# Sums of gated pairs, on GpSimd and VectorE or by accumulating transfers in DRAM

## The chip, the cores and the metric

The kernel runs on one core of a Trainium2 chip. A core has TensorE (PE in the profile, matmuls, with its weight loads PEld), VectorE (DVE), ScalarE (ACT) and GpSimd (POOL); SyncE (SP) issues the transfers in the kernel before. The metric is the device time of one execution in microseconds, lower is better.

## The reference

One encoder layer with shared weights is run on a prompt of 512 tokens and on a sample of 1024 tokens, in float32. After windowed attention, a convolution module and the output projection, both go through a gated feed-forward block, and this is the part that the change touches:

```python
h = _rmsnorm(x, norm_ffn_g[l])
u = _dwconv(h @ w_up[l], ffn_dw_w[l], ffn_dw_b[l])
x = x + (jax.nn.silu(u[..., :D_FF]) * u[..., D_FF:]) @ w_down[l]
...
return _rmsnorm(x, norm_final_g)
```

D_MODEL is 1024 and D_FF is 2816, which is 22 blocks of 128 columns. The output has to agree with this to nearly float32, so every matmul operand is split into a high part (float32r) and a low part (the rest), and each product is three matmuls: high by high, high by low, low by high.

## The kernel before

**Two feed-forward stages and one common last product.** The prompt's up-projection is a plain product: `ffn_step(k)` (line 1033) runs for each of the 22 blocks k, with two groups of 24 matmuls (lines 347, 348 and 350), the splitting of the next weights (`split`, line 227: the high half on ACT at line 230, the low half on GpSimd at line 231), the three taps of the convolution on DVE (line 969) and `gate(k)`. Meanwhile the sample's attention is woven in from a list of side jobs. Then follows the sample's output projection (lines 840 to 842), with transposes for norms (lines 816 and 1152) and further side jobs. The sample's up-projection is computed with seven products of half-size blocks in place of eight (Strassen's scheme in Winograd's form): `first` to `seventh` (lines 1307 to 1352), twelve matmuls each (lines 1229 to 1231). The down-projection (lines 1579 to 1581) is done for prompt and sample together, by the same scheme.

**The sums of a pair.** The seven products of the down-projection want, as their stationary operand, three blocks of the gated values as they are and four sums of blocks. Two neighbouring blocks of D_FF columns form a pair, 11 pairs in all. Call the even block's left and right token halves eL and eR, the odd block's oL and oR. Products 1, 2 and 4 use eL, oL and oR. Product 5 uses eR + oR, product 7 uses eL - eR, product 6 uses eR + oR - eL, and product 3 uses oL - (eR + oR - eL).

**Prompt.** `gate` (line 992) finishes a tile of 128 x 512 by a multiplication on GpSimd (line 1000), or on DVE for every fourth block, and stores it to `gt` in DRAM (line 1001). For pairs 7, 8 and 9 the sums are made at once by `pair_sums` (line 1013); for pairs 0 to 6 and the last one, `pair_sums` is a side job of the sample's output projection: it loads the pair again from `gt` (line 1016), makes four subtractions or additions of 128 x 256 on GpSimd (lines 1023, 1025, 1027, 1029) and stores the four results to `gb` (line 1030). The same GpSimd queue holds the two small operations of each norm's factor (`rstd_of`, lines 214 and 215).

**Sample.** The loop over j (line 1715) runs products of blocks j and j + 1 in a fixed order of TensorE's instructions: second(j), sixth(j), first(j+1), seventh(j), fifth(j+1), fourth(j), third(j). Between them stand the splits of the next block's weights (`split_up`, line 1200: high part on ACT at line 1215, low part on GpSimd through line 1092; split 7 reads a sum from a 2 KB tile), `value_part(j-1)` and `gate_part(j)`. `gate_part` takes the gate half through the convolution (lines 1357 to 1359) and a tanh (line 1366); `value_part` makes the gated product (line 1376), takes the value half through the convolution and multiplies (line 1378) into t, 128 x 1024. An even block's t is kept to the next step, and its left half is stored to `ga` (line 1383). With an odd block two halves are stored (line 1387), DVE makes the four sums of 128 x 512 (through lines 1089 and 1092), into the tiles x and e and a small one y, and SP stores them (line 1393). Copies of ACT between products (lines 1312, 1321, 1330, 1342) seed and drain the accumulators.

**Tiles.** `Slots` (line 74) gives out buffers of fixed classes: 15 q of 4096 bytes per partition, 4 c of 4224, 61 h of 2048, and some small ones. A request takes the smallest class that fits, and in it the buffer that came free first in program order. An instruction that writes a buffer waits until all that used it before, transfers included, have finished. `split_up` takes one 4 KB tile for high and low part if a q or c is free, and two h otherwise. Six of the q are reserved for the raw weights in the sample's stage.

**Order.** Where nothing is fixed by hand, a planner sets each engine's order of instructions at build time, by priority and by the times that it assumes; each engine then works through its own list in order. In the sample's up-projection TensorE's order is by hand, in the last product SP's too.

**The down-projection.** `load_next` (line 1491) fetches the operands ahead, from `ga` (line 1517), from `gt` or `gb` (lines 1512 and 1513) and from w_down. `evacuate` (line 1595) adds up the products as they end: u starts as product 1, o11 is u + product 2, e is product 5; then u takes product 6, o12 is u + e; u takes product 7, e takes u; u takes product 4. Product 3 goes into o12 at the end.

Of the kernel before, what the change touches and what calls it, by code (L numbers as in the profile page):

```python
# [9 lines left out]
F32 = mybir.dt.float32  # L10
# [3 lines left out]
ALU = mybir.AluOpType  # L14

P = 128
D = 1024
KC = D // P
NT = 512
# [154 lines left out]
def tile_hybrid_encoder(ctx: ExitStack, tc: tile.TileContext, xs, xsT, rel_bias, norm_attn_g, w_in,  # L174
                        attn_sink, w_out, norm_ffn_g, w_up, w_down, norm_final_g, packed, onehot, outs):
    nc = tc.nc
# [5 lines left out]
    dr = ctx.enter_context(tc.tile_pool(name="dr", bufs=1, space=bass.MemoryType.DRAM))  # L182
# [8 lines left out]
    sb = Slots(lambda tag: homes[tag[0]], dict(q=(15, 4096), c=(4, 4224), h=(61, 2048), d=(2, 2176), s=(32, 64)), "q", KEEP)  # L191
# [19 lines left out]
    ended = {}  # L211
# [99 lines left out]
    side, pace = deque(), dict(rate=0.0, due=0.0, conv=0.0, credit=0.0, late=0.0)  # L311
# [673 lines left out]
    NPAIR = NJ // 2  # L985
    HT = NT // 2
    gt = [dr.tile([P, 2, NT], F32, name=f"gt{p}") for p in range(NPAIR)]
    gb = [dr.tile([P, 4, HT], F32, name=f"gb{p}") for p in range(NPAIR)]
    GB = {5: 0, 7: 1, 6: 2, 3: 3}
    HL, HR = slice(0, HT), slice(HT, NT)  # L990

    def gate(j, a, b):
        th, t = bank("gate"), sb.tile([NT])
        nc.scalar.activation(th[:], a[:], AF.Tanh, scale=0.5)
        if j % 4 == VG:
            nc.vector.scalar_tensor_tensor(th[:], th[:], 1.0, a[:], op0=ALU.add, op1=ALU.mult)
            nc.vector.tensor_tensor(t[:], th[:], b[:], op=ALU.mult)
        else:
            nc.vector.scalar_tensor_tensor(t[:], th[:], 1.0, a[:], op0=ALU.add, op1=ALU.mult)
            nc.gpsimd.tensor_tensor(t[:], t[:], b[:], op=ALU.mult)  # L1000
        nc.sync.dma_start(gt[j // 2][:, j % 2, :], t[:])
        if j // 2 < SOON or j // 2 == NPAIR - 1:
            return
        if j % 2 == 0:
            evens[j // 2] = t
        else:
            for _ in pair_sums(j // 2, evens.pop(j // 2), t):
                pass

    evens = {}  # L1010
    SOON = 7

    def pair_sums(p, e=None, o=None):
        if e is None:
            g = sb.tile([2, NT], among="c")
            nc.sync.dma_start(g[:], gt[p][:])
            yield 0.0
            yield 0.0
            e, o = g[:, 0, :], g[:, 1, :]
        r = sb.tile([4, HT], among="c")  # L1020
        gp = nc.gpsimd.tensor_tensor
        with tc.issue_after(ended["pool"]):
            gp(r[:, 0, :], e[:, HR], o[:, HR], op=ALU.add)
        yield 0.0
        gp(r[:, 1, :], e[:, HL], e[:, HR], op=ALU.subtract)
        yield 0.0
        gp(r[:, 2, :], r[:, 0, :], e[:, HL], op=ALU.subtract)
        yield 0.0
        gp(r[:, 3, :], o[:, HL], r[:, 2, :], op=ALU.subtract)
        nc.sync.dma_start(gb[p][:], r[:])  # L1030
        yield 0.0

    def ffn_step(k):
        want_up_raw(k + 1, 1)
# [50 lines left out]
    W2 = 2 * NT  # L1085
    L, R = slice(0, NT), slice(NT, W2)

    def add(out, a, b, eng=None):
        (eng or nc.vector).tensor_tensor(out, a, b, op=ALU.add)  # L1089

    def sub(out, a, b, eng=None):
        (eng or nc.vector).tensor_tensor(out, a, b, op=ALU.subtract)  # L1092
# [153 lines left out]
            yield 0.0  # L1246

    side.extend((right_halves(), conv_norm(4 + NE)))
    side.extend(pair_sums(p) for p in (*range(SOON), NPAIR - 1))
    pace.update(rate=2.2)  # L1250
    for i in range(4, NB - 2):
        if i + NE + 1 < NB:
# [40 lines left out]
    def wide():  # L1293
        return wide_banks.tile([W2])

    ga = {(i, p): dr.tile([P, NT], F32, name=f"ga{i}_{p}") for i in range(1, 8) for p in range(NPAIR)}
    st = {}

    def pair_banks(j):
# [65 lines left out]
        t = s["t"] = sb.tile([W2])  # L1365
        nc.scalar.activation(t[:], ug[:], AF.Tanh, scale=0.5)

    even = {}

    def value_part(j):  # L1370
        if j < 0:
            return
        p = j // 2
        s = st.pop(j)
        ug, t = s["ug"], s["t"]
        nc.vector.scalar_tensor_tensor(t[:], t[:], 1.0, ug[:], op0=ALU.add, op1=ALU.mult)
        uv = dwconv(s.pop("wy"), NJ + j)
        nc.vector.tensor_tensor(t[:], t[:], uv[:], op=ALU.mult)
        del ug, uv
        s.clear()  # L1380
        if j % 2 == 0:
            even[p] = t
            nc.sync.dma_start(ga[1, p][:], t[:, L])
            return
        e, x, y = even.pop(p), sb.tile([W2]), sb.tile([NT])
        for i, blk in ((2, L), (4, R)):
            nc.sync.dma_start(ga[i, p][:], t[:, blk])
        add(x[:, R], e[:, R], t[:, R])
        sub(x[:, L], e[:, L], e[:, R])
        sub(e[:, R], x[:, R], e[:, L])  # L1390
        sub(y[:], t[:, L], e[:, R])
        for i, b in ((5, x[:, R]), (7, x[:, L]), (6, e[:, R]), (3, y[:])):
            nc.sync.dma_start(ga[i, p][:], b)

# [94 lines left out]
    def load_next(n):  # L1491
        for _ in range(n):
            if ahead:
                key, p = ahead.popleft()
                roomy = sum(f[0][0] in "qc" for f in sb.free) > 5
                if (key, p) in second_half:
                    t = second_half.pop((key, p))
                elif key in BRIEF and p % 2 == 0 and p + 1 < NPAIR and roomy:
                    both = sb.tile([2, NT])
                    t, second_half[key, p + 1] = Part(both, 0), Part(both, 1)  # L1500
                    both = None
                else:
                    t = sb.tile([NT])
                pr[key, p] = t
                what, i, n2 = key
                if what == "a":
                    src = ga[i, p][:]
                elif what == "g":
                    n = min(2, NPAIR - 2 * p)
                    for q in range(n):  # L1510
                        j, h = {1: (0, HL), 2: (1, HL), 4: (1, HR)}.get(i, (0, None))
                        src = gb[2 * p + q][:, GB[i], :] if h is None else gt[2 * p + q][:, j, h]
                        nc.sync.dma_start(t[:, q * HT:(q + 1) * HT], src)
                    continue
                else:
                    src = w_down[0, (2 * p + i) * P:(2 * p + i + 1) * P, n2 * NT:(n2 + 1) * NT]
                nc.sync.dma_start(t[:], src)
# [77 lines left out]
    def evacuate(i, w, z):  # L1595
        def at(name):
            return acc.setdefault(name, {})

        def fresh(name):
            t = at(name)[w] = sb.tile([W2])  # L1600
            return t

        if i == 1:
            nc.scalar.copy(fresh("u")[:], z[:])
        elif i == 2:
            add(fresh("o11")[:], z[:], acc["u"][w][:])
        elif i == 5:
            nc.scalar.copy(fresh("e")[:], z[:])
        else:
            u = acc["u"][w]  # L1610
            add(u[:], z[:], u[:])
            if i == 6:
                add(fresh("o12")[:], u[:], acc["e"][w][:], nc.gpsimd)
            elif i == 7:
                add(acc["e"][w][:], u[:], acc["e"][w][:], nc.gpsimd)

    def with_x(name, t, n):
        x = xd.pop((t, n))
# [227 lines left out]
```

## Time and profile before

| | |
|---|---|
| median of 3 runs | 1491.71 us |
| lowest and highest | 1491.32 and 1492.59 us |
| profiled execution | 1492.24 us, span 1490.4 us |
| prompt's gates (stores of line 1001) | 353.5 to 652.3 us |
| sample's stores of line 1393 | 795.1 to 1194.2 us |
| loads from `gb` | 1209.2 to 1431.6 us |
| transfers | 225.60 MB, mean 151 GB/s, all issued by SP |

The profile is of one execution. Its page gives, for each engine, the time in which it was busy; for TensorE the clock that was granted, here 1.00 in nearly every stage. A row of the timeline reads: start and length in us, engine, line, operation, output tile class <- input tile classes, shape, count, and in brackets how long the engine stood idle before it and what ended that. A row of the waits reads: engine, tile and line <- what it waited for, us in total, number of times, the longest. A row that groups instructions by line has the shortest, median and longest duration in ns and the first and last start in us. Rows of transfers end with the KB of one and the median us from issue to landing. Rows of the chain of work that ended last have start, us, and what.

### The profile page before, as it was taken

The numbers are of one execution on the slowest core, as the hardware profiler recorded it, in microseconds if no ns is written. First come the engines' busy times: TensorE is split into PE (matmuls) and PEld (weight loads), VectorE is DVE, ScalarE is ACT, GpSimd is POOL, SyncE is SP. The second block draws the span as 40 slices with busy tenths as digits, with TensorE's granted clock in tenths as the row PEclk, the third lists the DMA queues.
The fourth block names the chain that finished last, engine by engine and source line by source line (L and its number), as shares of the span: only waits on it lengthen the run. The fifth ranks groups of instructions, "written<-read, shape, count | busy, mean of one in ns | idle before, by whom it ended". The sixth has DMA issues, their size and how long they took to land.

```text
span 1490.4 us, 19857 instructions
## 1 busy us (share of the span) xinstructions
PE 1471.8 (99%) x6808; PEld 1218.8 (82%) x6808; DVE 1136.2 (76%) x1616; ACT 798.0 (54%) x1417; POOL 678.0 (45%) x540
## 2 busy tenths in 40 slices
PE   9999999999999999999999999999999999999998
PEld 7788887887888888878888888888887888888886
DVE  5999996888689975666868777777776945569884
ACT  8555656345777776444465544555445633444254
POOL 6962335235665575763326555555544000003345
PEclk9999999999999999999999999999999999999999
DMA  9953246374433347883213333333332672357644
GB/s 316 284 171 92 86 121 184 99 231 128 133 110 121 120 126 224 272 304 131 82 57 106 106 106 106 106 104 99 103 105 80 227 265 85 113 171 233 216 163 170
DMA packets 221905, 225.60 MB, mean 151 GB/s; under 512 B 12347, under 2 KB 161859, under 8 KB 221676
## 3 DMA queue, kind: packets, MB, share of 16 engines
q1 hardware_dynamic: 221804, 224.34, 47.0%
q8 instruction: 53, 0.87, 0.3%
q14 instruction: 48, 0.39, 0.1%
HBM read 165.29 MB, written 60.05 MB: 151 GB/s over the span
## 4 chain that ended last, share of the span: by engine, by line
PE 86%; DMA 5%; DVE 3%; POOL 2%; ACT 1%; issue 1%; SPq 0%; POOLq 0%; ACTq 0%; DVEq 0%
PE w L1229 9%; PE w L1231 9%; PE w L1230 9%; PE w L1580 7%; PE w L1579 7%; PE w L1581 7%; PE u L347 4%; PE u L348 4%; PE u L350 4%; PE b L347 4%; PE b L350 4%; PE b L348 4%; DMA c<-gt 2%; PE u L840 2%; PE u L842 2%; PE u L841 2%
## 5 line engine op out<-in xcount | busy, mean ns | idle before, releaser
L231 POOL TENSOR_TENSOR q<-q,q 128x1024 fp32r<-128x1024 f32 x71 | 172.9, 2439 | 122.8 <-ACT q L230 51.4
L1092 POOL TENSOR_TENSOR q<-q,q 128x512 fp32r<-128x512 f32 x101 | 141.5, 1408 | 151.2 <-ACT q L1215 140.3
L1092 DVE TENSOR_TENSOR h<-h,h 128x512 fp32r<-128x512 f32 (+2 forms) x202 | 157.4, 814 | 65.6 <-ACT h L1096 27.8
L1581 PE MATMUL w<-h,h 128*128 128x512 f32 x462 | 179.7, 389 | 0.0
L1579 PE MATMUL w<-h,h 128*128 128x512 f32 x458 | 178.2, 389 | 0.0
L1580 PE MATMUL w<-h,h 128*128 128x512 f32 x458 | 178.2, 389 | 0.0
L1229 PE MATMUL w<-h,q 128*128 128x512 f32 x448 | 174.9, 390 | 1.3 <-ACT w L1312 1.1
L1231 PE MATMUL w<-h,q 128*128 128x512 f32 x448 | 174.3, 389 | 0.0
L1230 PE MATMUL w<-h,q 128*128 128x512 f32 x426 | 165.8, 389 | 0.0
L402 DVE SCALAR_TENSOR_TENSOR c<-c,cvw,c 128x512 f32<-128x512 f32 x209 | 157.0, 751 | 3.1
L347 PE MATMUL u<-h,q 128*128 128x512 f32 x368 | 146.9, 399 | 1.9 <-DVE h L969 1.9
L348 PE MATMUL u<-h,q 128*128 128x512 f32 x368 | 144.0, 391 | 0.0
L350 PE MATMUL u<-h,q 128*128 128x512 f32 x360 | 141.2, 392 | 0.0
L1089 POOL TENSOR_TENSOR q<-q,q 128x1024 f32<-128x1024 f32 x12 | 33.1, 2772 | 229.4 <-DVE q L1089 212.9
L1096 ACT CAST h<-h 128x512 fp32r<-128x512 f32 x120 | 72.1, 622 | 97.1 <-DVE h L1092 40.5
L347 PE MATMUL b<-h,q 128*128 128x512 f32 x264 | 104.9, 397 | 0.9 <-DVE q L437 0.9
L230 ACT CAST q<-q 128x1024 fp32r<-128x1024 f32 (+1 forms) x73 | 75.7, 1041 | 54.5 <-POOL q L231 20.6
L348 PE MATMUL b<-h,q 128*128 128x512 f32 x264 | 103.7, 393 | 0.0
L350 PE MATMUL b<-h,q 128*128 128x512 f32 x264 | 103.5, 393 | 0.0
L1581 PEld LDWEIGHTS w<-h,h 128*128 128x128 f32 x462 | 86.7, 188 | 18.0
L1579 PEld LDWEIGHTS w<-h,h 128*128 128x128 f32 x458 | 86.0, 188 | 18.0
L1580 PEld LDWEIGHTS w<-h,h 128*128 128x128 f32 x458 | 86.0, 188 | 17.7
(443 smaller groups left out, 3625.1 us busy)
## 6 DMA issues: line engine op xcount, KB each, us to landing
q<-in_w_up SPq DMA_DIRECT2D x88, 512.0 KB, 4.3
ga<-q SPq DMA_DIRECT2D x64, 256.0 KB, 2.0
h<-ga SPq DMA_DIRECT2D x57, 256.0 KB, 3.4
q<-in_w_in SPq DMA_DIRECT2D x28, 512.0 KB, 5.1
h<-in_w_down SPq DMA_DIRECT2D x52, 256.0 KB, 4.0
q<-in_x_sample SPq DMA_DIRECT2D x15, 512.0 KB, 6.2
h<-qsd SPq DMA_DIRECT2D x23, 256.0 KB, 3.3
x1d<-q SPq DMA_DIRECT2D x11, 512.0 KB, 5.2
```

Of the source, the lines that this page charges most:

```text
L231: ins = (nc.vector if dve else nc.gpsimd).tensor_tensor(lo[:], raw[:], hi[:].bitcast(F32), op=ALU.subtract)
L347: nc.tensor.matmul(out, whi[:, kc, :], hi[:], start=(kc == 0), stop=False)
L348: nc.tensor.matmul(out, whi[:, kc, :], lo[:], start=False, stop=False)
L350: nc.tensor.matmul(out, wlo[:, kc, :], hi[:], start=False, stop=(kc == KC - 1))
L402: nc.vector.scalar_tensor_tensor(acc[:], src(t), w(t), acc[:], op0=ALU.mult, op1=ALU.add)
L1092: (eng or nc.vector).tensor_tensor(out, a, b, op=ALU.subtract)
L1229: nc.tensor.matmul(out, whi[:, s], hi[:], start=(start and c == 0), stop=False, **go)
L1230: nc.tensor.matmul(out, whi[:, s], lo[:], start=False, stop=False, **go)
L1231: nc.tensor.matmul(out, wlo[:, s], hi[:], start=False, stop=(stop and c == 3), **go)
L1579: nc.tensor.matmul(out, sh[:, c], th[:], start=(p == 0), stop=False)
L1580: nc.tensor.matmul(out, sh[:, c], tl[:], start=False, stop=False)
L1581: nc.tensor.matmul(out, sl[:, c], th[:], start=False, stop=(p == NPAIR - 1))
```

## The change

The four sums of a pair are no longer made by GpSimd (prompt) or DVE (sample). Each pair has one DRAM buffer of four parts, in the order of products 7, 6, 3, 5 (`gb`, and for the sample the new `gs`). With the even block SP writes eL to the parts 7, 6 and 3 and eR to the part 5, and a transfer from GpSimd adds eR to 7, 6 and 3. With the odd block a transfer from GpSimd adds oR to 6, 3 and 5, and another adds oL to 3. Since transfers only add, the second token half is treated as its negative: product 7 now uses eL + eR, 6 uses eL + eR + oR, 3 uses all four, and 5 uses eR + oR as before. The signs are put right in `evacuate`, with as many operations on the same engines. `pair_sums` with its reloads is gone, also from the list of side jobs, and so are `even`, x and y in `value_part`.

```diff
-    GB = {5: 0, 7: 1, 6: 2, 3: 3}
+    GB = {7: 0, 6: 1, 3: 2, 5: 3}
...
-        nc.sync.dma_start(gt[j // 2][:, j % 2, :], t[:])
-        if j // 2 < SOON or j // 2 == NPAIR - 1:
-            return
+        p = j // 2
+        nc.sync.dma_start(gt[p][:, j % 2, :], t[:])
         if j % 2 == 0:
-            evens[j // 2] = t
+            nc.sync.dma_start(gb[p][:, 0:3, :], three(t[:, HL]))
+            nc.sync.dma_start(gb[p][:, 3, :], t[:, HR])
+            into(gb[p][:, 0:3, :], three(t[:, HR]))
         else:
-            for _ in pair_sums(j // 2, evens.pop(j // 2), t):
-                pass
...
+            into(gb[p][:, 1:4, :], three(t[:, HR]))
+            into(gb[p][:, 2, :], t[:, HL])
+
+    def into(out, src):
+        nc.gpsimd.dma_start(out, src, accum_op=ALU.add)
+
+    def three(src):
+        return src.unsqueeze(1).to_broadcast([P, 3, src.shape[-1]])
...
-    side.extend(pair_sums(p) for p in (*range(SOON), NPAIR - 1))
...
+    gs = [dr.tile([P, 4, NT], F32, name=f"gs{p}") for p in range(NPAIR)]
+    GS = {7: 0, 6: 1, 3: 2, 5: 3}
...
         if j % 2 == 0:
-            even[p] = t
             nc.sync.dma_start(ga[1, p][:], t[:, L])
+            nc.sync.dma_start(gs[p][:, 0:3, :], three(t[:, L]))
+            nc.sync.dma_start(gs[p][:, 3, :], t[:, R])
+            into(gs[p][:, 0:3, :], three(t[:, R]))
             return
-        e, x, y = even.pop(p), sb.tile([W2]), sb.tile([NT])
         for i, blk in ((2, L), (4, R)):
             nc.sync.dma_start(ga[i, p][:], t[:, blk])
-        add(x[:, R], e[:, R], t[:, R])
-        sub(x[:, L], e[:, L], e[:, R])
-        sub(e[:, R], x[:, R], e[:, L])
-        sub(y[:], t[:, L], e[:, R])
-        for i, b in ((5, x[:, R]), (7, x[:, L]), (6, e[:, R]), (3, y[:])):
-            nc.sync.dma_start(ga[i, p][:], b)
+        into(gs[p][:, 1:4, :], three(t[:, R]))
+        into(gs[p][:, 2, :], t[:, L])
...
-                    src = ga[i, p][:]
+                    src = gs[p][:, GS[i], :] if i in GS else ga[i, p][:]
...
             u = acc["u"][w]
-            add(u[:], z[:], u[:])
             if i == 6:
-                add(fresh("o12")[:], u[:], acc["e"][w][:], nc.gpsimd)
+                sub(u[:], u[:], z[:])
+                sub(fresh("o12")[:], u[:], acc["e"][w][:], nc.gpsimd)
             elif i == 7:
-                add(acc["e"][w][:], u[:], acc["e"][w][:], nc.gpsimd)
+                add(u[:], z[:], u[:])
+                sub(acc["e"][w][:], acc["e"][w][:], u[:], nc.gpsimd)
+            else:
+                sub(u[:], z[:], u[:])
```

More of the change, by code (lines that the diff above doesn't have):

```diff
@@ L1000, in gate @@
             nc.gpsimd.tensor_tensor(t[:], t[:], b[:], op=ALU.mult)
-        nc.sync.dma_start(gt[j // 2][:, j % 2, :], t[:])
-        if j // 2 < SOON or j // 2 == NPAIR - 1:
-            return
+        p = j // 2
+        nc.sync.dma_start(gt[p][:, j % 2, :], t[:])
         if j % 2 == 0:
-            evens[j // 2] = t
-        else:
-            for _ in pair_sums(j // 2, evens.pop(j // 2), t):
-                pass
[L1010 to L1031, printed above, removed]
+            nc.sync.dma_start(gb[p][:, 0:3, :], three(t[:, HL]))
+            nc.sync.dma_start(gb[p][:, 3, :], t[:, HR])
+            into(gb[p][:, 0:3, :], three(t[:, HR]))
+        else:
+            into(gb[p][:, 1:4, :], three(t[:, HR]))
[4 more added lines that the diff above has]
+        return src.unsqueeze(1).to_broadcast([P, 3, src.shape[-1]])
     def ffn_step(k):
@@ L1294, in wide @@
         return wide_banks.tile([W2])
-    ga = {(i, p): dr.tile([P, NT], F32, name=f"ga{i}_{p}") for i in range(1, 8) for p in range(NPAIR)}
+    ga = {(i, p): dr.tile([P, NT], F32, name=f"ga{i}_{p}") for i in (1, 2, 4) for p in range(NPAIR)}
+    gs = [dr.tile([P, 4, NT], F32, name=f"gs{p}") for p in range(NPAIR)]
+    GS = {7: 0, 6: 1, 3: 2, 5: 3}
     st = {}
@@ L1366, in gate_part @@
         nc.scalar.activation(t[:], ug[:], AF.Tanh, scale=0.5)
-    even = {}
     def value_part(j):
```

## The prediction

> **What bounds the kernel now.** I read the page's busy times first, then TensorE's waits from 352 us on (the first gate's store, line 1001, is issued at 353.5 us), then the windows of the two feed-forward stages.
>
> ```profile
> PE 1471.8 (99%) x6808; PEld 1218.8 (82%) x6808; DVE 1136.2 (76%) x1616; ACT 798.0 (54%) x1417; POOL 678.0 (45%) x540
> PE u L347 <- DVE h L969: 1.3, 2, 0.7
> PE w L1229 <- ACT w L1312: 1.1, 1, 1.1
> PE a L816 <- DVE h L810: 1.0, 2, 0.5
> PE w L1229 <- ACT w L1330: 0.3, 1, 0.3
> PE t L1152 <- DVE h L1092: 0.2, 1, 0.2
> 400.00:450.00 50.00, 50.00 (x244) 42.02 (x243) 42.93 (x83) 36.38 (x70) 30.61 (x19) 1.00 0.38 119
> 900.00:950.00 50.00, 50.00 (x222) 41.42 (x221) 37.20 (x36) 24.95 (x35) 24.16 (x17) 1.00 0.32 103
> ```
>
> TensorE is busy 99% of the span at a granted clock of 1.00, and the change leaves its matmuls as they are. A window row gives the length, then the busy us of PE, weight loads, DVE, ACT and POOL, then clock, DMA share and GB/s: in the prompt's stage (400 to 450) and the sample's (900 to 950) PE has no gap at all. All its waits from 352 us on add up to 1.3 + 1.1 + 1.0 + 0.3 + 0.2 = 3.9 us, of which the first L347 wait (0.6 us, at 352.2) lies before any step that changes. So the most that lighter engines can give back is 3.3 us, 0.2% of 1491.7 us. A loss has no such limit: it comes when a cover that is now long enough becomes too short. The question is therefore only which waits appear.
>
> **What goes away.**
>
> ```profile
> L1023 POOL TENSOR_TENSOR c<-c x8: 730/738/748, 618.7 to 668.1; 128x256 f32<-128x256 f32 x8
> L1092 DVE TENSOR_TENSOR h<-q,q x11: 679/692/694, 843.3 to 1194.2; 128x512 f32<-128x512 f32 x10, 128x512 fp32r<-128x512 f32 x1
> 670.58 0.74 POOL c L1029
> 671.32 0.52 POOL rs L215
> 671.86 1.28 DVE q L1110
> ...
> 677.52 0.73 DVE h L810
> 678.25 0.14 issue
> 678.39 0.63 PE a L816 x4
> ...
> 1121.67 0.85 DVE q L1376
> 1122.54 0.62 ACT q L1215
> 1123.16 0.49 ACT h L1321
> 1123.64 1.12 ACT q L1357
> 1124.79 1.29 DVE q L1358
> 1126.11 1.29 DVE q L1359
> 1127.50 0.58 ACT w L1312
> ```
>
> Prompt: 11 pairs by 4 GpSimd operations of 0.738 us (x8 row) are 32.5 us of POOL, with eight reloads and eleven stores of 512 KB. Sample: 44 DVE operations of 0.692 us are 30.4 us of DVE, with 44 stores on SP. Neither engine sets the pace, so I count only the PE waits whose chain runs through them. The first chain goes from a sum (L1029) over the norm's factor (L215) and the row scaling to the transposes of L816: this wait and its twin at 655.7 go, 1.0 us. The second goes from the gate product (L1376) over a cast held up in ACT's queue (L1215) to the seed copy (L1312); the cast writes a tile that this product has just read. One more free 4 KB tile, which the change leaves (no x, and the even gate isn't kept for a whole step), relieves that: 1.1 us. Together 2.1 us; I take 2.0. The waits on L347 at 617 us and on L1330 have no such chain and stay.
>
> **What comes instead, in the sample's stage.** For an even step SP issues the store of ga, then two stores to gs (768 KB and 256 KB); GpSimd issues a 768 KB accumulation when these have landed. For an odd step GpSimd issues 768 KB, waits until that has landed because the 256 KB of the next one lie on the same rows, and issues those. No arithmetic on an engine is added; what matters is how long the gated tile t stays held. Tiles of 4 KB are given out again in the order in which they came free. Reading the code: after an even step the free ones are the gate half's tile and then t, so split 6 of the next block takes the first and split 7 takes t. Today t is kept until the odd step, and split 7 takes a tile that a matmul has released. The trace confirms this order in an odd step, where split 7 (the cast from an h tile) waits for a store of the sums:
>
> ```profile
> 898.35 2.31 DVE L1378 TENSOR_TENSOR q<-q,c 128x1024 f32<-128x1024 f32 x1
> 896.70 0.62 ACT L1215 CAST q<-h 128x512 fp32r<-128x512 f32 x1
> 900.68 0.34 SPq L1383 DMA_DIRECT2D ga<-q  x1
> 915.19 0.39 PE L1231 MATMUL w<-h,q 128*128 128x512 f32 x1
> 917.66 0.57 ACT L1330 COPY w<-w 128x512 f32<-128x512 f32 x1 [1.57 <-PE w L1231]
> 921.50 0.62 ACT L1215 CAST q<-h 128x512 fp32r<-128x512 f32 x1 [0.72 <-DMA ga<-q]
> L1092 POOL TENSOR_TENSOR q<-h,q x22: 1287/1300/1743, 749.2 to 1153.6; 128x512 fp32r<-128x512 f32 x22
> ga<-q SPq DMA_DIRECT2D x64, 256.0 KB, 2.0
> gb<-c SPq DMA_DIRECT2D x11, 512.0 KB, 4.0
> x1d<-c SPq DMA_DIRECT2D x1, 512.0 KB, 2.6
> ```
>
> In the even step shown, t is finished at 898.35 + 2.31 = 900.66 us, and the cast of split 7 ran already at 896.70. Its weights are wanted by the seventh product of the next step, which ends at the copy of 917.66; its third matmul, at 915.19, is the first to use the low part. Going back 1.30 us of POOL and 0.62 of ACT, the cast may start as late as **913.3 us**. The new holder of t reads as follows. Stores: issued from 900.68, 0.34 us apart, so the 768 KB go out at 901.0. No row is that large; by 2.0 us for 256 KB and 2.6 for 512 it is 3.2, by 4.0 for 512 it is 6.0; 1.25 MB are under way together, so I take 4.4, landing at 905.4. GpSimd's issue appears nowhere: from SP's 0.34 to three times 1.30 (one pass of POOL over each third); I take 1.3, its one row of that size, until 906.7. The accumulation is a read and a write of 768 KB: from 3.2 us (wholly overlapped) to 12.0 (twice 6.0, one after the other); I take the middle, 7.6, since two weight loads of 512 KB are under way in the same microseconds (DMA share 0.32). It lands at 914.3, **1.0 us too late**. The bounds are 907.8 (5.5 us to spare) and 901.0 + 6.0 + 3.9 + 12.0 = 922.9 (9.6 late). Ten even steps have a following split 7, so this costs 10 us. Behind the cast ACT holds L1312 and L1330, which come later anyway.
>
> In an odd step the next gate's tile is t, and it would come some 5 to 7 us later than now. The product that uses it runs a step later, and the DVE queue is shorter by four operations; I take nothing for it, and 1.5 us per step (15 in all) if that slack is used up.
>
> **In the prompt's stage** the work on GpSimd is the risk.
>
> ```profile
> L1001 SPq DMA_DIRECT2D gt<-h x22: 319/339/1007, 353.5 to 652.3; - x22
> 443.44 2.40 POOL L231 TENSOR_TENSOR q<-q,q 128x1024 fp32r<-128x1024 f32 x1
> 450.34 2.40 POOL L231 TENSOR_TENSOR q<-q,q 128x1024 fp32r<-128x1024 f32 x1 [0.75 <-ACT h L731]
> 450.04 0.39 PE L347 MATMUL u<-h,q 128*128 128x512 f32 x1
> 458.29 0.39 PE L347 MATMUL u<-h,q 128*128 128x512 f32 x1
> ```
>
> 22 gates from 353.5 to 652.3 us make 14.2 us a step, 28.5 a pair; POOL is busy 30.61 of 50 us, so 11 us a pair are free. Three accumulations at 1.3 us take 3.9. The low halves of the weights are finished at 445.84 and 452.74, for groups of matmuls that start at 450.04 and 458.29: covers of 4.2 and 5.5 us. An issue at the head of POOL that waits (even: for SP's stores; odd: for the accumulation before it) holds up everything behind it, the low halves first. The planner puts ready work ahead of a waiting issue, and the tiles are half as large as the sample's, so the real wait exceeds the planned one by less than the cover: I cost it at nothing. If an odd step's wait exceeds the cover by 2 us, eleven pairs cost 22 us. The extra stores raise a DMA share of 0.38, far from full. After 600 us the eight reloads disappear.
>
> **The sum** is made against the profiled execution, 1492.2 us (its span is 1490.4), 0.5 above the median: 1492.2 - 2.0 + 10 = 1500.2, by the median **1499.7**, slower by 0.5%.
>
> **The rivals.** *Not slower*: the accumulation in an even step lands by 913.3 us, which it does if issue and transfer together take under 7.9 us behind the stores instead of my 8.9. For it speaks that the one quiet store of 512 KB took 2.6 us; against it, the loads in the same stretch. All waits are then covered and only the 2.0 us remain: 1489.7, within 0.2%. *Faster*: the same, and every wait that can go does, 3.3 us: 1488.4. Nothing in the trace ties the L347 and L1330 waits to the sums. *POOL held in the prompt's stage*: the 22 us above without the sample's loss, 1511.7; for it speaks the cover of 4.2 us, against it 11 idle us a pair. *Half rate*: reading and writing the destination don't overlap, the transfer takes 12.0 us and lands at 918.7, 5.4 us late ten times: 1543.7. [...] No row here has such a transfer. That the change doesn't do what it says is hardly possible, since the later loads read only what these transfers write.
>
> **Chances.** Forecast 0.37, not slower 0.34, faster 0.07 (of which 0.05 is more than 0.2%), POOL held 0.11, half rate 0.11. A measurement of this kernel can tell about 0.2%, 3.0 us, from no change (the runs shown spread over 1.3 us). So faster 0.05, same 0.34 + 0.02 = 0.36, slower 0.37 + 0.11 + 0.11 = 0.59. The forecast's own range is 1495 to 1530 (a lateness of 0.6 to 4 us ten times). The range of 8 in 10 reaches down to the not slower case, 1489, and up to 1530; half rate, half of faster and a small rest lie outside.
>
> **What would show it.** Forecast: a wait of PE on POOL or ACT at L1229 to L1231 every 38 us in the sample's stage, in front of a seventh product, and a cast at L1215 released by an accumulation into gs; PE stays without gaps from 400 to 600 us. POOL held: waits of PE at L347 to L350 on POOL L231. Not slower: PE's waits stay under 4 us and those at L816 and L1312 are gone. Wrong altogether would be a POOL issue that lasts several times 1.3 us, since it would load both stages at once, or a new wait in the last product, where I see no edit that costs anything: the two kinds of additions there keep their engines and shapes.

## The result, and the profile after

| | |
|---|---|
| before, median of 5 runs | 1492.59 us |
| after, median of 5 runs | 1612.55 us (1611.4 to 1617.16) |
| ratio after to before | 1.0812, 95% interval 1.0792 to 1.0832 |
| profiled execution after | 1617.16 us, span 1615.4 us, mean clock 0.969 |

The changed kernel is slower by 120 us, where 8 were predicted. The profiled execution of one kernel below (e4) took 6075 us against 1603 to 1608 in its other three, so its trace is not read and its median is that of those three.

The first rows are the busy times from the page of the changed kernel, then TensorE's waits (us in total, times, the longest), then the two windows that were shown of before. Line numbers moved: 1213 to 1215 are the products (before 1229 to 1231), 1199 the cast of a split (1215), 1076 its low half (1092), 1297 and 1306 the copies behind the first and sixth product (1312, 1321), 1342 and 1344 the first and the last tap of the convolution (1357, 1359), 1012 the accumulations.

```profile
PE 1520.7 (94%) x6808; PEld 1242.0 (77%) x6808; DVE 1089.2 (67%) x1572; ACT 791.9 (49%) x1417; POOL 709.0 (44%) x562
...
PE w L1213 <- DVE q L1344: 23.2, 4, 8.4
PE w L1215 <- POOL q L1076: 17.1, 14, 1.5
PE w L1213 <- ACT q L1199: 12.6, 9, 2.4
PE u L840 <- ACT h L230: 8.6, 2, 8.4
...
400.00:450.00 50.00, 46.57 (x209) 37.39 (x208) 36.41 (x68) 29.63 (x57) 30.28 (x20) 0.93 0.52 130
900.00:950.00 50.00, 46.44 (x201) 37.06 (x200) 27.60 (x27) 20.82 (x31) 23.56 (x19) 1.00 0.49 116
```

VectorE is lighter, as intended (1136.2 to 1089.2 us). But TensorE now has gaps in both stages: span less busy time was 18.6 us and is 94.7 (76 us more). And it is busy 49 us longer (1471.8 to 1520.7) with the same 6808 matmuls, at a mean granted clock of 0.969 where it was 0.998 (the last section shows the clock falling to 0.50 for some microseconds at a time). Both add up to the 125 us by which the span grew.

How much of it lies in the sample's stage is read from the seed copy behind each first product, one per step. The rows are that copy of before and of after, with the first and last start:

```profile
L1312 ACT COPY w<-w x20: 570/570/570, 786.5 to 1146.5; 128x512 f32<-128x512 f32 x20
```

```profile
L1297 ACT COPY w<-w x20: 570/570/587, 818.6 to 1269.4; 128x512 f32<-128x512 f32 x20
```

360.0 us in 19 steps are 18.95 us a step before, 450.8 are 23.73 after: on average a step is 4.8 us longer, 91 us in all, where the forecast had 1.0 us in every second one. It is not spread evenly. By the starts of this copy, two steps near the stage's start (832.98 to 893.34 us) are 22 us longer together and the last two (1215.75 to 1269.45) 13; of the 14 between, those with an even gated tile are longer by 3.3 us on average and those with an odd one by 4.6. Yet the sizes that the forecast had estimated were close. From the transfers' part of the page and the row of the accumulations' issues:

```profile
gs<-q POOLq DMA_DIRECT2D x21, 768.0 KB, 7.7
gs<-q SPq DMA_DIRECT2D x11, 768.0 KB, 3.6
L1012 POOL DMA_DIRECT2D gs<-q x31: 887/1297/1335, 831.2 to 1320.5; - x31
```

The accumulation of 768 KB lands 7.7 us after its issue starts (taken: 1.3 for the issue and 7.6 behind it, 8.9), GpSimd's issue takes 1.30 us, the store 3.6 us (taken: 4.4). What was wrong is who waits for them. The timeline of the changed kernel, an even step (t is finished at 1009.4) and then an odd one:

```profile
1013.89 1.30 POOL L1012 DMA_DIRECT2D gs<-q  x1 [2.51 <-PE w L1215]
1021.59 0.62 ACT L1199 CAST q<-h 128x512 fp32r<-128x512 f32 x1 [6.23 <-DMA gs<-q]
1022.11 0.61 ACT L1199 CAST q<-q 128x512 fp32r<-128x512 f32 x1
1022.78 0.50 PE L1213 MATMUL w<-h,q 128*128 128x512 f32 x1 [1.02 <-ACT q L1199]
1024.85 0.50 PE L1215 MATMUL w<-h,q 128*128 128x512 f32 x1 [1.34 <-POOL q L1076]
...
1032.58 1.30 POOL L1012 DMA_DIRECT2D gs<-q  x1 [1.98 <-DVE q L1362]
1041.59 0.92 POOL L1012 DMA_DIRECT2D gs<-q  x1 [6.38 <-DMA gs<-q]
1042.22 2.85 POOL L1076 TENSOR_TENSOR q<-q,q 128x512 fp32r<-128x512 f32 x2
1045.74 0.62 ACT L1199 CAST q<-h 128x512 fp32r<-128x512 f32 x1 [7.46 <-issue]
1046.26 0.61 ACT L1199 CAST q<-q 128x512 fp32r<-128x512 f32 x1
1046.93 0.50 PE L1213 MATMUL w<-h,q 128*128 128x512 f32 x1 [2.24 <-ACT q L1199]
1049.00 0.79 PE L1215 MATMUL w<-h,q 128*128 128x512 f32 x1 [1.34 <-POOL q L1076]
```

The cast from an h tile is split 7; it writes t's buffer, so it starts when the accumulation has landed (1013.89 + 7.7 = 1021.6). Until then ScalarE stands for 6.2 us. Directly behind it in ScalarE's queue stands a cast of another split (q<-q at 1022.11), for which TensorE waits 1.0 us; the low half of that split then stands behind split 7's on GpSimd, and TensorE waits another 1.3 us. In the odd step GpSimd's second issue (1041.59) first waits 6.4 us for the landing of the first, and the cast comes 13.2 us after the first issue (the profile names nothing that released it; that it takes t's buffer is shown by the planned order of e2 below). So the odd step is the worse one, and it was taken as nothing.

The largest of TensorE's waits, the 23.2 us behind the last tap, are four, one in each of the four longest steps. The longest is at 887.84:

```profile
881.23 1.20 ACT L1342 ACTIVATE q<-w,vecs,fw 128x1024 f32<-128x1024 f32 x1 [5.26 <-DMA gs<-q]
886.43 1.27 DVE L1344 SCALAR_TENSOR_TENSOR q<-w,fw,q 128x1023 f32<-128x1023 f32 x1
887.84 0.77 PE L1213 MATMUL w<-h,q 128*128 128x512 f32 x1 [8.42 <-DVE q L1344]
```

Here the first tap of a gate takes a buffer with an accumulation under way, and the taps behind it come late. The wait at 1263.91 (5.4 us) is of the same kind; those at 857.31 and 1236.53 (4.9 and 4.5 us) follow an issue of GpSimd that itself waited 5.5 and 6.6 us.

These rows show two queues that stand still at once: ScalarE's at an instruction that takes t's buffer, mostly a cast (theory T1), and GpSimd's at issues that wait for an earlier landing, with low halves behind them (rival R2). A second rival, R3, was that the load of the transfers themselves delays others.

### The profile page after: what moved, and what is told of

It is laid out like the page before. It is cut to its first block, busy times and chain, and to the rows that moved or that the text cites. A ratio compares the mean times of both kernels' runs of the same rounds, so it can differ in the third digit from the quotient of the medians.

```text
span 1615.4 us, 19877 instructions
## 1 busy us (share of the span) xinstructions
PE 1520.7 (94%) x6808; PEld 1242.0 (77%) x6808; DVE 1089.2 (67%) x1572; ACT 791.9 (49%) x1417; POOL 709.0 (44%) x562
## 4 chain that ended last, share of the span: by engine, by line
PE 65%; DMA 11%; issue 8%; POOL 7%; DVE 6%; ACT 2%; SPq 0%; POOLq 0%; DVEq 0%; ACTq 0%
PE w L1561 6%; PE w L1560 6%; PE w L1562 6%; DMA gs<-q 5%; PE u L347 4%; PE u L348 3%; PE u L350 3%; PE b L347 3%; PE b L350 3%; PE b L348 3%; POOL q L1076 3%; PE w L1213 3%; PE w L1215 3%; PE w L1214 3%; DMA gb<-h 3%
## 5 line engine op out<-in xcount | busy, mean ns | idle before, releaser
L1076 POOL TENSOR_TENSOR q<-q,q 128x512 fp32r<-128x512 f32 (+1 forms) x115 | 172.6, 1551 | 271.6 <-DMA h<-gb 148.2
L1213 PE MATMUL w<-h,q 128*128 128x512 f32 x480 | 198.8, 414 | 37.0 <-DVE q L1344 18.3
L231 POOL TENSOR_TENSOR q<-q,q 128x1024 fp32r<-128x1024 f32 x71 | 178.6, 2521 | 83.3 <-ACT q L230 50.3
L1215 PE MATMUL w<-h,q 128*128 128x512 f32 x480 | 197.1, 411 | 17.1 <-POOL q L1076 17.1
L1214 PE MATMUL w<-h,q 128*128 128x512 f32 x458 | 186.7, 408 | 0.0
L347 PE MATMUL u<-h,q 128*128 128x512 f32 x368 | 150.7, 410 | 8.2 <-DVE h L969 7.9
L350 PE MATMUL u<-h,q 128*128 128x512 f32 x360 | 144.1, 400 | 2.7 <-POOL q L231 2.7
L348 PE MATMUL u<-h,q 128*128 128x512 f32 x368 | 146.3, 397 | 0.0
L1213 PEld LDWEIGHTS w<-h,q 128*128 128x128 f32 x480 | 95.4, 199 | 66.0 <-ACT q L1199 22.2
L1215 PEld LDWEIGHTS w<-h,q 128*128 128x128 f32 x480 | 95.6, 199 | 43.8 <-POOL q L1076 23.1
L230 ACT CAST q<-q 128x1024 fp32r<-128x1024 f32 (+1 forms) x73 | 75.4, 1039 | 73.7 <-POOL q L231 40.3
L1214 PEld LDWEIGHTS w<-h,q 128*128 128x128 f32 x458 | 91.5, 200 | 18.8
L350 PE MATMUL b<-h,q 128*128 128x512 f32 x264 | 103.5, 393 | 0.0
L1562 PEld LDWEIGHTS w<-h,h 128*128 128x128 f32 x462 | 86.7, 188 | 18.0
```

The lines of the kernel that those rows point to most:

```text
L231: ins = (nc.vector if dve else nc.gpsimd).tensor_tensor(lo[:], raw[:], hi[:].bitcast(F32), op=ALU.subtract)
L347: nc.tensor.matmul(out, whi[:, kc, :], hi[:], start=(kc == 0), stop=False)
L348: nc.tensor.matmul(out, whi[:, kc, :], lo[:], start=False, stop=False)
L350: nc.tensor.matmul(out, wlo[:, kc, :], hi[:], start=False, stop=(kc == KC - 1))
L1213: nc.tensor.matmul(out, whi[:, s], hi[:], start=(start and c == 0), stop=False, **go)
L1214: nc.tensor.matmul(out, whi[:, s], lo[:], start=False, stop=False, **go)
```

## The experiments

All ratios are to before in the same series; its medians were 1490.5 to 1491.8 us.

| | median us | ratio, 95% interval |
|---|---|---|
| e1 signs only | 1490.5 | 0.9998 (0.9988 to 1.0008) |
| e2 sample's part only | 1578.4 | 1.0590 (1.0574 to 1.0606) |
| e3 prompt's part only | 1524.1 | 1.0220 (1.0203 to 1.0236) |
| e4 all, tile kept a step | 1607.5 | 1.0774 (1.0751 to 1.0797) |
| e5 sample, tile kept a step | 1575.8 | 1.0569 (1.0548 to 1.0590) |
| e9 sample, tile kept two steps | 1578.2 | 1.0584 (1.0566 to 1.0602) |
| e12 as e9, casts fixed | 1561.4 | 1.0478 (1.0454 to 1.0502) |
| e6 sample, issued late | 1526.4 | 1.0231 (1.0214 to 1.0248) |
| e10 as e6, kept a step longer | 1535.1 | 1.0293 (1.0275 to 1.0312) |
| e13 as e10, casts fixed | 1497.7 | 1.0049 (1.0031 to 1.0068) |
| e14 signs only, casts fixed | 1492.3 | 1.0010 (1.0000 to 1.0020) |
| e8 as e2, no add | 1504.4 | 1.0090 (1.0070 to 1.0110) |
| e17 as e13, no add | 1491.4 | 1.0007 (0.9998 to 1.0017) |
| e11 prompt, issued late | 1503.2 | 1.0083 (1.0058 to 1.0108) |
| e16 as e3, no add | 1498.3 | 1.0060 (1.0043 to 1.0077) |
| e7 both issued late | 1542.5 | 1.0351 (1.0332 to 1.0371) |
| e15 e11 and e13 together | 1511.1 | 1.0132 (1.0109 to 1.0154) |

**The parts (e1, e2, e3).** In e1 both `gate` and `value_part` make the sums on the engines again, with the new signs; e2 does so for the prompt alone, e3 for the sample alone:

```diff
-        gp(r[:, 1, :], e[:, HL], e[:, HR], op=ALU.subtract)
+        gp(r[:, 1, :], e[:, HL], e[:, HR], op=ALU.add)
...
-        sub(x[:, L], e[:, L], e[:, R])
+        add(x[:, L], e[:, L], e[:, R])
```

> The signs of the second half are turned, but all sums are made by GpSimd and VectorE as before, with additions in place of subtractions. Theory T1 (the gated tile, held by its accumulations, is taken at once by split 7, whose cast stands in ACT's queue ahead of the next copies) and the rivals R2 (GpSimd's queue, blocked by accumulations that wait for earlier ones, holds up the low halves directly) and R3 (the transfers themselves are a load that delays others): all expect no change, 1488 to 1496 us. If the signs or the last product had a part in the loss, it would be above 1500.

> The prompt's sums are made by GpSimd again, the sample's by accumulating transfers. T1: the loss of the sample's stage stays, 21 steps by some 4 us and the late gates at its start, 1570 to 1600 us; about 20 to 30 us of the 120 go with the prompt's. R3, with the load as the cause: also 1570 to 1600. Under any theory in which the prompt's accumulations are what GpSimd drags along into the sample's stage it would fall below 1550.

> The sample's sums are made by VectorE again, the prompt's by accumulating transfers. T1: 1505 to 1525 us, since the only loss left is the one between 345 and 690 us. R2: the prompt's stage has three accumulations a step pair on GpSimd as the sample's has, so it should show PE waits on L231; above 1530 if R2 is the main cause.

The signs cost nothing. The sample's part costs 5.90% (88 us), the prompt's 2.20% (33 us), somewhat more than was expected, and their sum is the whole (8.12%). So each can be studied alone.

**Keeping the tile (e4, e5, e9).** The gated tile is held for one step more (two in e9) before its buffer is given out; e4 does so with the whole change, e5 and e9 with the sample's part alone:

```diff
         s.clear()
+        kept.append(t)
+        del kept[:-1]
         if j % 2 == 0:
```

> As after, but the sample's gated tile is kept for one more step before its buffer is given out, so that split 7 takes a tile whose transfers were issued some 19 us earlier. T1: the casts at L1199 no longer wait for gs transfers for more than 1 us, PE's waits at L1213 and L1215 behind ACT go, and the time falls to 1505 to 1535 us (the prompt's loss stays). R2: GpSimd's queue is as before, above 1590. R3: the transfers are the same, above 1590.

> [...] e4 took nearly all of T1's claim: keeping the tile gained only 5 us. R2 now says that the low halves on GpSimd stand behind accumulations that wait: PE's waits at L1235 to L1237 behind POOL L1098 grow to more than 40 us in all while those behind ACT's casts released by gs transfers vanish, 1565 to 1580 us. If T1 held for the sample's stage after all, 1495 to 1515.

> As e5, the sample's tile kept two steps instead of one. In e5 the casts still waited 119 us for gs transfers: split 7 runs early in its step and the tile given to it was only some 12 us old, so e4 and e5 did not take away what T1 names. Two steps make it some 30 us old. T1 as the main cause: ACT's waits on gs transfers under 15 us, the time 1500 to 1530 us. R2 as the main cause (GpSimd's order is as in e2, 78 us of waits): 1555 to 1580 us.

All three miss T1's numbers and lie within R2's. But the traces of e5 and e9 show that the edit didn't take away what T1 names, so they don't decide between the two. ScalarE's waits in e5, and in e9:

```profile
ACT q L1221 <- DMA gs<-q: 119.0, 16, 11.0
```

```profile
ACT q L1221 <- DMA gs<-q: 59.5, 11, 7.2
```

The reason is in the planned order of GpSimd, which is fixed at build time (position, line, destination <- source):

```
e2
 411 L1034 DMA gs3_7616<-q0_1348_8943 128x3x512
 413 L1034 DMA gs3_7616<-q0_1348_8943 128x512
 416 L1098 TENSOR_TENSOR q0_1359_9064<-h41_1353_8986
e9
 396 L1034 DMA gs2_7615<-q10_1322_8663 128x3x512
 398 L1034 DMA gs2_7615<-q10_1322_8663 128x512
 400 L1098 TENSOR_TENSOR q10_1359_9064<-h41_1353_8986
e12
 393 L1034 DMA gs2_7615<-q10_1322_8663 128x3x512
 395 L1034 DMA gs2_7615<-q10_1322_8663 128x512
 411 L1098 TENSOR_TENSOR q10_1359_9064<-h41_1353_8986
```

The last row of each is the low half of the split 7 that takes the tile's buffer (q0 in e2, q10 in the others). In e2 it stands 3 instructions behind the last accumulation. In e9 the program asks for it two steps later, but split 7's input, the third sum, is ready early, and the planner puts the split where it expects the buffer to be free: 2 instructions behind. The wait moves along with the tile. A cast that isn't needed yet then blocks ScalarE's queue.

**Fixing the casts (e12, e14).** Each cast is tied behind the accumulator copy that stands before it in the program; e12 is e9 with this, e14 is e1 with this:

```diff
+            with (tc.issue_after(ended["copy"]) if "copy" in ended else nullcontext()):
-            nc.scalar.copy(hi[:], src)
+                nc.scalar.copy(hi[:], src)
```

> As e9, and each cast of a split is fixed behind the accumulator copy that stands before it in the program, so that the planner can't pull it forward. In the planned order of GpSimd the next writer of a tile stood 2 to 4 instructions behind the accumulation in e9 (3 to 5 in e2), here it stands 16 to 18 behind, more than two steps. That takes T1 away at last; GpSimd's accumulations still wait where they did. T1 as the main cause: ACT's waits on gs transfers near 0 and the time 1495 to 1525 us. R2 as the main cause: above 1555.

> Control: no accumulation (as e1), the casts fixed as in e12 and e13. All theories: 1488 to 1496 us; what it loses beyond that is the price of fixing the casts and has to be taken off e12 and e13.

Fixing costs nothing that can be told (1.0010). In e12 no cast waits for a gs transfer any more, but the time falls only to 1561 us: of the 88 us, T1 alone gives back 17. The other queue is enough to keep the rest. The timeline of e12:

```profile
987.50 1.29 POOL L1034 DMA_DIRECT2D gs<-q  x1
996.08 0.92 POOL L1034 DMA_DIRECT2D gs<-q  x1 [5.06 <-DMA gs<-q]
996.71 4.08 POOL L1098 TENSOR_TENSOR c<-q,c 128x512 fp32r<-128x512 f32 x3
999.58 5.05 DVE L1098 TENSOR_TENSOR q<-q 128x512 f32<-128x512 f32 x2 [3.77 <-POOL c L1098]
1006.99 1.28 DVE L1368 SCALAR_TENSOR_TENSOR c<-w,fw,c 128x1023 f32<-128x1023 f32 x1
1008.38 0.57 ACT L1321 COPY w<-w 128x512 f32<-128x512 f32 x1 [7.91 <-DVE c L1368]
1009.01 0.79 PE L1236 MATMUL w<-h,q 128*128 128x512 f32 x1 [4.13 <-ACT w L1321]
```

GpSimd stands for 5 us at the 256 KB accumulation. Behind it are three low halves; VectorE's sums overwrite the raw weights that these read, so they wait; behind those sums stands the last tap (L1368), which reads the accumulator that the seed copy (L1321) needs; and TensorE stands for 4.1 us. So the wait passes through two other engines' work before it reaches a matmul. That is R2, by a longer way than it was stated; it is the longest of ten waits of TensorE on this copy, 22.6 us in all. The time is in the range that was given for R2 as the main cause.

**Issuing late (e6, e10, e13).** Each accumulation is issued at the end of a step, behind that step's last low half; the three of a pair are a step apart each, so that none waits for the one before. e6 keeps the tile one step beyond its last issue; e10 one more, with split 7 in 2 KB tiles; e13 is e10 with the casts fixed.

```diff
-            into(gs[p][:, 0:3, :], three(t[:, R]))
+            later.add(0, t, lambda: into(gs[p][:, 0:3, :], three(t[:, R])))
...
-        into(gs[p][:, 1:4, :], three(t[:, R]))
-        into(gs[p][:, 2, :], t[:, L])
+        later.add(0, t, lambda: into(gs[p][:, 1:4, :], three(t[:, R])))
+        later.add(1, t, lambda: into(gs[p][:, 2, :], t[:, L]))
...
         split_up(j + 1, 3)
+        later.step()
...
-        split_up(j + 1, 7)
+        split_up(j + 1, 7, apart=True)
```

(The last change in e10 and e13 alone.)

> As e5, and each accumulation is issued at the end of a step, behind the last low half of that step, the three of a pair one step apart each (even; odd by three parts; odd's single part), with the tile kept one step beyond its last issue. The transfers, their bytes and their number are the same; only GpSimd waits no more for what came before. R2 and T1 together: GpSimd's waits on gs transfers fall from 78 us to under 10 and the time to 1490 to 1505 us. R3, the load of the transfers themselves: it stays above 1560.

> As e6, the tile kept one step longer after its last accumulation was issued (split 7 takes two 2 KB tiles, to make room). In e6 GpSimd waits little, but casts of splits 1 and 2 still waited 28 us for gs transfers, with the seed copy L1320 behind them. If T1 and R2 together are all of the sample's loss: 1488 to 1500 us. If the load of 20 MB of accumulations has a part of its own, it stays at 1515 to 1530.

> As e10 (issued late, kept one more step, split 7 in 2 KB tiles), with the casts fixed as in e12: the next writer stands 13 to 31 instructions behind the accumulation. Neither GpSimd nor ACT waits for a gs transfer in the steps any more. T1 and R2 together: 1488 to 1502 us. If the load has a part of its own: 1510 to 1535.

Waits of GpSimd in e2, then in e6; and of ScalarE and TensorE in e6:

```profile
POOL gs L1034 <- DMA gs<-q: 78.4, 17, 10.0
```

```profile
POOL gs L1034 <- DMA gs<-q: 50.4, 5, 13.5
ACT q L1221 <- DMA gs<-q: 28.3, 7, 6.3
PE w L1235 <- ACT w L1320: 21.8, 10, 3.6
```

Of the five waits left on GpSimd in e6 one is at the stage's start (5.1 us, until 822.87) and four lie after 1200 us, where the last pair's accumulations follow one another; in the steps between it waits no more. That gives 52 us. The time lies between the ranges of both theories: casts still take tiles with accumulations under way, and the seed copy stands behind them. Keeping the tile longer (e10) moved these waits and made it 9 us worse, slower than either of its two ranges. With both queues free in the steps, e13 is 1497.7 us, 5.4 above e14, which has no accumulation. 81 of 88 us are gone. T1 alone gave 17, R2 alone (with part of T1) 52: each, left alone, keeps much of the loss.

**The add itself (e8, e17).** Plain transfers from GpSimd of the same bytes to the same rows, in the order of e2 and of e13:

```diff
-        nc.gpsimd.dma_start(out, src, accum_op=ALU.add)
+        nc.gpsimd.dma_start(out, src)
```

> The sample's accumulations are replaced by plain transfers of the same bytes from GpSimd's queue to the same rows, so the sums are left out; all waits on GpSimd stay, only the transfer is shorter if the add costs anything. A 768 KB accumulation lands in 7.7 us where SP's 768 KB store takes 3.6 us. If the length of the accumulation is what makes the waits, the loss of 88 us falls by about half, to 1520 to 1550 us; if the queue or the order is all, it stays at 1565 to 1580.

> As e13 (1497.7 us, no waits for gs transfers in the steps), with plain transfers in place of the accumulations; the sample's sums are left out. e14, without any such transfer, takes 1492.3. If the 5 us between them are the load of the accumulations (DMA share 0.6 against 0.3), it falls to 1490 to 1494 us; if they are the price of the order (issues on GpSimd, split 7 in 2 KB tiles, the last pair's accumulations), it stays at 1496 to 1500.

GpSimd's issues (shortest, median, longest in ns), the queue of its transfers (packets, MB, share of 16 engines' span) and their size and landing, in e2 and then in e8:

```profile
L1034 POOL DMA_DIRECT2D gs<-q x31: 884/1297/1524, 798.1 to 1283.0; - x31
q0 software_dynamic: 10384, 20.19, 8.6%
gs<-q POOLq DMA_DIRECT2D x21, 768.0 KB, 7.6
```

```profile
L1034 POOL DMA_DIRECT2D gs<-q x31: 552/767/1003, 797.6 to 1203.3; - x31
q0 software_dynamic: 5456, 20.19, 3.4%
gs<-q POOLq DMA_DIRECT2D x21, 768.0 KB, 4.3
```

Without the add the same chain of waits has links of 4.3 us in place of 7.6 and issues of 0.77 in place of 1.30, and 74 of the 88 us vanish: more than the half that was expected, so the waits don't shrink in proportion to the transfer; that the rest is covered by slack is the likely reason, not a measured one. e17 against e13 tells what the accumulations cost where engines should hardly wait for them: 6.3 us. e17 lies in the range that was given for the load, so this is the upper end of R3's part; but most of it is R2 again. In e13:

```profile
822.87 1.29 POOL L1034 DMA_DIRECT2D gs<-c  x1 [8.13 <-DMA gs<-q]
825.51 0.50 PE L1238 MATMUL w<-h,q 128*128 128x512 f32 x1 [4.05 <-POOL q L1223]
```

At the stage's start GpSimd stands 8.1 us for the first pair's accumulation, a low half stands behind it, and TensorE stands 4.1 us; e17 has no such wait (TensorE's longest there is 1.7 us). That leaves 2.2 us, at a mean granted clock of 0.997 in e13 against 0.999 in e17. How much of them is the load itself was not shown; they are less than the runs scatter (1496.75 to 1501.45 us in e13, 1489.38 to 1494.58 in e17).

**The prompt (e11, e16), and all together (e7, e15).** e11 issues the prompt's accumulations late by the same means and keeps the tile three gates longer; e16 is e3 with plain transfers; e7 is both stages late (the sample's as in e6, the prompt's tile kept one gate beyond its last issue), e15 is e11 and e13.

> The prompt alone by accumulations (e3: 1524 us), each issued a gate later than now, the odd single part two gates later, and the tile kept three gates beyond its last issue. If the prompt's loss is of the same kind as the sample's (GpSimd standing, tiles given out with accumulations under way): 1490 to 1503 us. If it is the load (the DMA share is 0.63 to 0.91 from 340 to 700 us in e3, 0.38 before): 1512 to 1528 us.

> As e3 (the prompt alone), its accumulations replaced by plain transfers of the same bytes from GpSimd's queue to the same rows, so the sums of the prompt are left out; order and waits stay. In the sample's stage this took 74 of 88 us away (e8). If the length of the accumulation makes the prompt's loss as well: 1493 to 1505 us against 1524 in e3. If the loss is in what GpSimd's issue costs or in tiles that are held: 1512 to 1525.

> The whole change, with the accumulations issued late in both stages (the prompt's each one gate later than now, behind a low half of the weights, the odd single part two gates later). R2: both losses go, 1490 to 1510 us. R3: above 1590. If only the sample's loss comes from GpSimd's waits, 1515 to 1530.

> The whole change with the prompt's accumulations as in e11 and the sample's as in e13. If the losses add: the prompt's 12 us of e11 on top of e13, 1498 to 1515 us. It would beat before only if the accumulations themselves cost nothing and the 3.3 us of waits that lighter engines can give back come in: below 1489.

GpSimd's waits at its accumulations, ScalarE's largest wait for them and TensorE's two largest in e3, then GpSimd's in e11:

```profile
POOL gb L1012 <- DMA gb<-h: 37.1, 13, 6.6
ACT h L230 <- DMA gb<-h: 14.8, 1, 14.8
PE u L347 <- DVE h L969: 12.0, 4, 4.7
PE u L840 <- ACT h L230: 9.4, 2, 8.1
```

```profile
POOL gb L1038 <- DMA gb<-h: 17.6, 5, 6.6
```

The prompt's loss looks to be of the same kind: late issues with longer kept tiles give back 21 of 33 us (e11, at the upper end of its first range), the shorter transfer 26 (e16). The two queues were not separated here. The load did not go with the time: from 340 to 700 us the mean DMA share is 0.52 in before, 0.68 in e3 (0.54 to 0.91 in windows of 50 us) and 0.72 in e11. TensorE's waits come through the last tap and a cast; directly on a low half at L350 it waits only 2.4 us in e3. What is left, 12 us in e11 and 8 in e16, was not taken apart; ScalarE's waits for gb transfers at L230 are still 19.6 us in e11. e7's loss of 52 us, between the ranges of all three theories, is about that of e6 (35) and of e11 (12) together. e15 is the whole change in the best form that was tried: 1511 us, 1.3% slower than before, as expected if the losses of e11 and e13 add. No form of it was faster. e17, which spares VectorE the sums and hardly waits, is no faster than before (interval 0.9998 to 1.0017), so the lighter VectorE brought nothing that shows.

## Why the prediction was wrong

- **Bounds and gains.** That the question was only which waits appear held. Of the 2.0 us that were taken off as a gain no run shows anything: e17 is at 1.0007.
- **Terms.** The forecast did not fail by a duration. Issue and transfer of the accumulation took 7.7 us together against 8.9, the store 3.6 against 4.4. Put into the forecast's own chain these give a landing at 901.0 + 3.6 + 7.7 = 912.3 us, before its deadline of 913.3. So the condition of *not slower* (under 7.9 us) was met, and by the forecast's own account the change should have cost nothing. That it called the direction right is luck.
- **"Behind the cast ACT holds L1312 and L1330, which come later anyway"** is the first step that failed. The deadline of 913.3 us was split 7's own, a whole product away. In the trace of before, three copies, three activations of the gate and four other casts already stood on ScalarE between this cast (896.70) and that deadline. In the changed order the cast of another split stands directly behind it, and TensorE waits for that one (1022.11 and 1022.78 us). Here the latest start of the instruction that waits was set by what stood behind it in its queue, not by its own reader. Casts released by accumulations, the forecast's sign, did come (44.1 us in 9 waits), but they were not what cost most: with these waits gone (e12) 17 of 88 us come back.
- **"In an odd step the next gate's tile is t ... I take nothing for it"** failed too. In the odd step as well t's buffer goes to split 7 (2 to 5 instructions behind the accumulations in the planned order of e2, pairs 1 to 8), two accumulations in a row must land, and the cast starts 13.2 us after the first issue. It is the dearer of the two steps. And where a gate does take t's buffer (881.23), TensorE stands for 8.4 us.
- **GpSimd's queue was weighed for the prompt alone**, and this left out the largest part. For the sample's stage the forecast has no such term, though the same sentence, that a waiting issue holds up all behind it, applies there: e12 against e13 shows it to be worth 64 us once the casts are fixed (e13 also gives split 7 its own 2 KB tiles).
- **The slower clock was no term at all**, though TensorE's busy time grew by 49 of the span's 125 us, at a mean granted clock of 0.969 against 0.998.
- **The rivals.** *POOL held in the prompt's stage* had 22 us; the prompt's part cost 33 (e3), and the window from 400 to 450 us, which was to stay without gaps, has some. But its sign, waits of TensorE on L231, came to only 2.4 us at L350: the waits reach TensorE through VectorE and ScalarE. *Half rate* had 12.0 us for the transfer behind its issue, 13.3 with it, and the sample's loss at 54 us; issue and transfer took 7.7, and the loss was larger by another way. On the same queue the transfer landed 7.6 us after its issue with the add and 4.3 us without (e2, e8), 1.8 times as long. That an accumulation reads and writes its 768 KB, from which the forecast's 7.6 us and this rival's 12.0 were worked out, was the author's estimate: no row shows the second read, and the pages of e2 and e8 both count 165.29 MB read.

## What to carry to other kernels

When a transfer from a compute engine's queue replaces arithmetic, list for each wait that it adds all that stands behind the waiting instruction on that engine, and follow it through the other engines' queues to the next matmul; an instruction's own deadline says little. A buffer that is held longer does not help if a planner gives it out again at the moment at which it believes it free: look at how many instructions stand between the last reader and the next writer in the planned order, and fix that. Where gaps of TensorE crowd together, look at the granted clock behind them: in the odd step above 3.6 us of gaps went with 6.8 us at a clock of 0.50, in which TensorE was busy for 5.5 us. Its matmuls started 0.43 us apart there (from 1049.59 to 1054.28) and 0.23 apart after it, so an estimate of the cost is 5.5 x 0.20 / 0.43 = 2.6 us.

## What the runs showed of the hardware

**The clock fell after short gaps.** Windows of the changed kernel: four around the odd step above, two around a later step, one at the even step above (the busy time of TensorE is the second number; clock and DMA share are the last but two and last but one):

```profile
1044.21:1047.63 3.42, 1.18 (x5) 0.35 (x3) 0.00 (x0) 1.89 (x3) 2.06 (x2) 1.00 0.82 209
1047.63:1051.04 3.41, 2.07 (x6) 1.66 (x6) 3.03 (x4) 1.30 (x2) 1.31 (x2) 0.50 0.48 143
1051.04:1054.45 3.41, 3.41 (x10) 2.63 (x9) 3.41 (x4) 2.19 (x4) 2.69 (x2) 0.50 0.00 0
1054.45:1057.87 3.42, 3.42 (x17) 2.79 (x16) 2.25 (x3) 1.11 (x2) 1.00 (x2) 1.00 0.17 63
...
1139.79:1143.20 3.41, 1.64 (x6) 1.06 (x7) 1.88 (x3) 2.44 (x3) 2.45 (x2) 1.00 0.87 259
1143.20:1146.61 3.41, 3.41 (x10) 2.66 (x9) 3.41 (x4) 2.00 (x4) 1.55 (x2) 0.50 0.03 7
...
1020.32:1023.73 3.41, 2.17 (x9) 1.16 (x7) 0.00 (x0) 2.14 (x3) 1.45 (x2) 1.00 1.10 314
```

In this trace the clock changes only at times that lie a multiple of 3.41 us apart (its stretches at 0.50 last 3.41, 6.83 or 10.24 us, but for one that the end cuts off), and these windows are cut there. The clock falls to 0.50 behind the first gap of the odd step (2.24 us, from 1044.69), before the second one, and stays there for two windows, 6.8 us. Here it went with how the gaps lay in such a window, not with their length alone: behind gaps of 0.74 and 1.34 us, nearly all of them in one window (busy 1.64), it is 0.50 from 1143.20, while behind the longer pair of the even step, 1.02 and 1.34 us, which lies across two (busy 2.17 and 2.30), it stays at 1.00. In the whole of this trace the 17 windows at 1.00 with up to 1.64 us of work were followed by 0.50, and none of those with 1.93 us or more was. That is what one trace shows; what sets the clock no row tells.

**The accumulating transfers took longer than plain ones of the same bytes.** For the same 20.19 MB (rows of e2 and e8 above) they made about twice the packets (10384 against 5456) and took the engines 2.65 times as long (8.6% of 1576 us against 3.4% of 1502); GpSimd's issue took 1.30 in place of 0.77 us (medians). In the prompt's stage (e3, e16) it is 10384 against 2992 packets for 10.09 MB, and 2.9 times the time (4.8% of 1522 us against 1.7% of 1496).
